# Transposed decode weights go back into their row tile, and the feed-forward's right factors start 192 bytes lower

## The chip, the cores and the metric

The kernel runs on one core of one Trainium2 chip. The metric is the device time of one launch in microseconds (us). A core has a matrix engine (PE, whose weight loads are listed apart as PEld), a vector engine (DVE), a scalar engine (ACT), a general engine (POOL) and a queue processor (SP) that issues nearly all DMA transfers here. Each engine runs its own list of instructions in order, and waits for the others by semaphores. About 0.2% of the time, 3.7 us, is what a measurement of this kernel can tell from no change.

## What is computed

One step of one transformer-like layer over 1024 new frames of a prompt stream and 8 cached streams of 16 new frames each, T = 1152 rows of width 1024, all float32:

```python
def layer(h, p, past, mk, mv):
    mix, st = mixers(rmsnorm(h, p['norm_mix_g']), p, past)
    h = h + mix
    h = h + cross_attend(rmsnorm(h, p['norm_x_g']), mk, mv, p['wq_x'], p['wo_x'])
    h = h + swiglu(rmsnorm(h, p['norm_ffn_g']), p['w_gate'], p['w_up'], p['w_down'])
    return h, st
```

`mixers` projects the rows by `w_in` and runs three mixers side by side: stick-breaking attention (4 heads of 64), a state-space scan (SSD, 8 heads, chunks), and forgetting attention (FoX: softmax attention with cumulated forget gates, 4 heads). The cached streams attend to 1024 past rows, whose keys and values lie in `cache_fox_k`, `cache_fox_v` (and `cache_sb_k`, `cache_sb_v`):

```python
def fox_attend(q, k, v, fq, fk, q_pos, k_pos):
    s = jnp.einsum('bqhd,bkhd->bhqk', q, k) * (HEAD_DIM ** -0.5)
    s = s + (transpose(fq)[..., :, None] - transpose(fk)[..., None, :])
    valid = k_pos[None, :] <= q_pos[:, None]
    p = softmax(where(valid, s, -inf))
    return jnp.einsum('bhqk,bkhd->bqhd', p, v)
```

`swiglu(u)` is `silu(u @ w_gate) * (u @ w_up) @ w_down` with an inner width of 2816.

## The kernel before

The stages follow one another on PE: the memory projection, the norm, the projections by `w_in`, the two attentions (stick-breaking, m = 0; FoX, m = 1) woven with what is left of the projections and then with the SSD chunks, the output projection, cross attention, gate and up, and down. Matrix products of float32 accuracy are made of three matmuls on rounded high and low parts (L341 to L343, and L1918).

No hand-written order: the program text emits the instructions, and a scheduler that simulates the engines chooses each engine's order from the dependencies, the free buffers and priorities. So a change in what holds a buffer moves instructions on all engines, also where their own code is the same.

The buffers that matter here come from pools. `actp` has 6 tiles of 128 x 3072 float32 (`act` in the trace). `wsp` has 7 tiles of 128 x 1152 (`ws`): a tile holds one block of attention rows, that is the scores and then the weights of 128 queries against all keys. `stp` has 8 smaller ones (`st`), and `so` is a pool of 4.

**The cached streams' units.** For each m there are four (p = 0 to 3, two streams each). A unit has a first part `rows` (L869): the queries go in block form into `qt`, cached keys are loaded (L894), transposed on PE (L900) and copied by ACT (L902, `kf`), scores are taken (L885), and the softmax is done (L544 to L555, in a `ws` tile). Its second part `av` (L925) transposes the weights in pieces of 128 x 128 (PE, L936), copies them from PSUM (ACT, L937) to `wt` (past) and `wn` (new rows), and multiplies them with the cached values (loaded by L954; PE, L945). For m = 0 `qt` and `wt` are tiles of `st`, and `wn` a tile of its own; for m = 1 all three are columns of one whole `act` tile, `hold`, which `rows` takes and `av` lets go.

**The SSD scan.** `ssd_gen` (L982) takes one `act` tile, `sc`, for its constants (columns up to 2456), then for each of nine chunks an `act` tile A, into which `load` brings three things: the projected inputs (L1049, `xbcsc`), the cumulated decay spread over all partitions (L1051, `acsc`), and the gate `z` (L1053, `zsc`). ACT and DVE turn the decay into factors (L1089, L1091, L1094), PE multiplies (L1066, L1070, L1081, L1106, L1112, L1151, L1168), and `write` transposes the chunk's output (L1180), copies it (ACT, L1181, `sg`) and stores it (L1182). Other names in the change's neighbourhood: L573, L574, L576 are score matmuls of the prompt's FoX rows, L591 their weights' transposes, L606 their products with the values, L619 the store of these.

**Gate and up** multiply seven sums of the activations (left factors, stationary, `tr`, `tl`, `st`) by seven prepared sums of the normalised rows (right factors `b` and `bT`, moving), 3696 matmuls at L1918, half of them 256 columns wide and half 320. Before the pools of the right factors a small tile `gap` is allocated, so its size shifts the address of everything allocated behind it.

Of the kernel before, what the change touches and what calls it, by code (L numbers as in the profile page):

```python
# [8 lines left out]
F32 = mybir.dt.float32  # L9
# [8 lines left out]
P = 128  # L18
# [5 lines left out]
PAST = 1024  # L24
# [39 lines left out]
def tile_hybrid_step(ctx: ExitStack, tc: tile.TileContext, a: dict):  # L64
# [22 lines left out]
    def act_t(dt=F32R, home=None):  # L87
        return (home or actp).tile([P, 3072], dt, tag="act", name="act")
# [4 lines left out]
    def st_t(dt=F32R):  # L93
        return stp.tile([P, 1024], dt, tag="st", name="st")
# [526 lines left out]
    def sg2_t(dt=F32):  # L621
        return ptp.tile([P, 256], dt, tag="so", name="so", bufs=4)
# [226 lines left out]

    def decode_units(m):
        ck = (a["cache_sb_k"], a["cache_fox_k"])[m][0].rearrange("b k h d -> b k (h d)")
        cv = (a["cache_sb_v"], a["cache_fox_v"])[m][0].rearrange("b k h d -> b k (h d)")
        dmask = dmask_fx if m else dmask_sb
        new = []

        def load_new():

            qsm = st_t(F32).rearrange("p (i x t) -> p i x t", i=4, x=2)  # L860
            SP.dma_start(out=qsm.rearrange("p i x t -> p (i x) t"),
                         in_=f32(qk_sc[4 * m:4 * m + 4, :, :, SEQ:T]).rearrange("i x p t -> p (i x) t"))
            POOL.tensor_tensor(out=qsm[:, :, 0, :], in0=qsm[:, :, 0, :], in1=qsm[:, :, 1, :], op=ALU.add)
            vsm = pt_t(F32)[:, :256].rearrange("p (h x d) -> p h x d", h=4, x=1)
            SP.dma_start(out=vsm.rearrange("p h x d -> p (h x d)"), in_=v_sc[m][SEQ:T, :])
            new.extend((qsm, vsm))

        def rows(p):
            if not new:  # L869
                load_new()  # L870
            qsm = new[0]

            hold = act_t(F32) if m else None
            qt = (hold if m else st_t(F32))[:, 0:P]
            POOL.memset(qt, 0.0)
            q0 = qsm[:, 0:2, 0, 32 * p:32 * p + 32].rearrange("p n (b t) -> p n b t", b=2)
            qp = qt.rearrange("p (b n e t) -> p n e b t", b=2, n=2, e=2)
            for par in range(2):
                r = slice(par * 64, par * 64 + 64)
                for nb in range(2):  # L880
                    POOL.tensor_copy(qp[r, nb, par], q0[r, nb])

            def quads(ps, moving):

                together([lambda g=g: PE.matmul(ps[32 * g:32 * g + 32, :], qt[:, 32 * g:32 * g + 32],  # L885
                                                moving(g // 2, g % 2), start=True, stop=True) for g in (3, 0, 1, 2)])

            def load_k(hf, b2):
                rvs = []
                for q in range(2):  # L890
                    rvs.append(raw_t()[:, :512].rearrange("p (k c) -> p k c", c=256))
                    k0 = hf * 512 + q * 256

                    SP.dma_start(out=rvs[q], in_=ck[2 * p + b2, k0:k0 + 256, :].rearrange("(p k) c -> p k c", k=2))  # L894
                kf = ring.tile([P, 1088], F32, tag=("wh", "wl")[b2], name="kf")
                for q in range(2):
                    tp = pT()
                    for nb in range(2):
                        for k in range(2):
                            PE.transpose(tp[:, (2 * nb + k) * P:(2 * nb + k + 1) * P], rvs[q][:, k, nb * P:(nb + 1) * P],  # L900
                                         ident)
                    ACT.copy(kf[:, :1024].rearrange("c (n q p k) -> c n q p k", n=2, q=2, k=2)[:, :, q],  # L902
                             tp.rearrange("c (n k p) -> c n p k", n=2, k=2))
                return kf

            def emit_past(hf):
                def emit(ps):
                    kf = [load_k(hf, b2) for b2 in range(2)]
                    quads(ps, lambda b2, nb: kf[b2][:, nb * 512:(nb + 1) * 512])
                return emit  # L910

            def emit_new(ps):
                PE.matmul(ps, identr, dmask[:, 96 - 32 * p:224 - 32 * p], start=True, stop=False)
                together([lambda g=g: PE.matmul(ps[32 * g:32 * g + 32, :], qt[:, 32 * g:32 * g + 32], qsm[:, 2 + g % 2, 0, :],
                                                start=False, stop=True) for g in range(4)])

            pieces = [(0, 512, emit_past(0)), (512, 512, emit_past(1)), (1024, P, emit_new)]
            if m == 0:
                return sb_rows(T, pieces), hold
            fkb = xc_t()  # L920
            SP.dma_start(out=fkb[:, :PAST],
                         in_=fs4[8 * p:8 * p + 8].rearrange("r i k -> (r i) k").unsqueeze(1).to_broadcast([32, 4, PAST]))
            return fox_rows(T, pieces, [(0, PAST, fkb[:, :PAST]), (PAST, P, fnew)], fqs[:, p:p + 1], frs[:, p:p + 1]), hold

        def av(p, w, hold):  # L925
            vsm = new[1]

            wt = hold[:, P:P + 1024] if m else st_t(F32)
            wn = hold[:, P + 1024:2 * P + 1024] if m else sg2_t()[:, :P]
            for k0 in (0, 4, 8):  # L930
                nk = min(4, 9 - k0)
                tp = pT()
                for k in range(nk):
                    wk = w[:, 8 * P:9 * P] if k0 == 8 else \
                        w[:, k0 * P:(k0 + 4) * P].rearrange("q (p k) -> q p k", k=4)[:, :, k]
                    PE.transpose(tp[:, k * P:(k + 1) * P], wk, ident)  # L936
                ACT.copy(wn if k0 == 8 else wt[:, k0 * P:(k0 + 4) * P], tp[:, :nk * P])  # L937

            po = pO()

            def quads(w, moving, start, stop):
                def one(g):
                    v = moving(g // 2, g % 2)
                    out = po[32 * g:32 * g + 32, :P]
                    return PE.matmul(out if len(v.shape) == 2 else out.rearrange("p (h d) -> p h d", h=2),  # L945
                                     w[:, 32 * g:32 * g + 32], v, start=start, stop=stop)
                return [lambda g=g: one(g) for g in (3, 0, 1, 2)]

            work = quads(wn, lambda b2, nb: vsm[:, 2 * nb:2 * nb + 2, 0, :], True, False)
            for hf in range(2):  # L950
                raws = []
                for b2 in range(2):
                    raw = ring.tile([P, 1088], F32, tag=("wh", "wl")[b2], name="vr")
                    SP.dma_start(out=raw[:, :1024].rearrange("p (k c) -> p k c", c=256),  # L954
                                 in_=cv[2 * p + b2, hf * 512:(hf + 1) * 512, :]
                                 .rearrange("(p k) c -> p k c", k=4))
                    raws.append(raw)
                for k in range(4):
                    work += quads(wt[:, (4 * hf + k) * P:(4 * hf + k + 1) * P],
                                  lambda b2, nb, raws=raws, k=k: raws[b2][:, k * 256 + nb * P:k * 256 + (nb + 1) * P],  # L960
                                  False, hf == 1 and k == 3)
            together(work)
            ob = sg2_t()[:, :P]
            DVE.scalar_tensor_tensor(ob.rearrange("p (h d) -> p h d", h=2), po[:, :P].rearrange("p (h d) -> p h d", h=2),
                                     frs[:, p:p + 1] if m else 1.0, maskh.unsqueeze(2).to_broadcast([P, 2, 64]),
                                     ALU.mult, ALU.mult)
            of = pT()
            PE.matmul(of[:, :64], ob, fold2.rearrange("p n t -> p (n t)"), start=True, stop=True)
            on = sg2_t()[:, :64]
            DVE.tensor_copy(on, of[:, :64])  # L970
            SP.dma_start(out=mix_sc[2 * m:2 * m + 2, :, SEQ + 32 * p:SEQ + 32 * p + 32].rearrange("n p t -> p n t"),
                         in_=on.rearrange("p (n t) -> p n t", n=2))

        return [([lambda p=p: rows(p)], lambda w, p=p: av(p, *w[0])) for p in range(4)]


    final = []

    def ssd_gen():
        sc = act_t(F32)  # L980
        hT, gB = sc[:, 0:512], sc[:, 512:1024]
        triu, btri, ones, bones = (sc[:, 1024 + 128 * i:1152 + 128 * i] for i in range(4))  # L982
        bmask = sc[:, 1536:1544]
# [736 lines left out]
    tmp = ctx.enter_context(f_pool("tmp", 1))  # L1720
    tlp = ctx.enter_context(f_pool("tlp", NL))
    gap = ctx.enter_context(f_pool("gap", 1))
    gap.tile([P, 56], F32, tag="gap", name="gap")
    bstack = ctx.enter_context(ExitStack())
    slots = [(tlp, "tl")]
    turn = [0]
# [398 lines left out]
```

## Time and profile before

| what | value |
| --- | --- |
| time, median of 3 runs | 1868.5 us (1866.71 to 1868.78) |
| time of the profiled execution | 1863.43 us |
| its span | 1861.7 us |
| mean granted PE clock | 0.992 |
| PE busy | 1804.3 us, 97% |
| DVE / ACT / POOL busy | 897.6 / 796.8 / 619.4 us |
| DMA, mean | 156 GB/s |

A page of the profile gives each engine's busy time, the span in 40 slices (each 46.5 us here) with the busy tenths, the granted clock of PE (9 is 90% or more) and the DMA share, and the chain of work that ended last. Views of the trace give the waits by engine (who waited for what, for how long), the instructions in order of time, and stretches with busy time and clock. In a row of the order of time, equal instructions that follow one another are merged ("x4"), and a bracket shows how long the engine stood idle ahead of them and what ended that. The stretch of the two attentions woven with SSD runs from about 200 to 720 us.

### The profile page before, as it was taken

Reading aid. Unit: us, or ns where it says so; the run is one execution under the profiler, and the core shown is the slowest. Engines: PE = TensorE matmul, PEld = TensorE weight load, DVE = VectorE, ACT = ScalarE, POOL = GpSimd, SP = SyncE. Lnnn points to the kernel's source line nnn. Section 1 sums busy time; section 2 is a strip of 40 time slices with the busy share of each in tenths; the row PEclk is TensorE's granted clock in tenths of the full one; section 3 lists DMA queues with packets and bytes.
Section 4 is the critical chain, followed back from the end, with each engine's and each line's share of the span. In section 5 each row is a group of like instructions: output and inputs, shape, how many; then the busy total and the mean of one; then the engine's idle time right before and its main releaser. Section 6 shows DMA issues by size and latency. Waiting matters only on the chain.

```text
span 1861.7 us, 32061 instructions
## 1 busy us (share of the span) xinstructions
PE 1804.3 (97%) x12008; PEld 1617.0 (87%) x12008; DVE 897.6 (48%) x1792; ACT 796.8 (43%) x1697; POOL 619.4 (33%) x921
## 2 busy tenths in 40 slices
PE   7999999999999999999999989999999999999998
PEld 5899878888966777899988889999999999888886
DVE  3412323476657864455553695333333334455554
ACT  6532544545456862343342564333333333344443
POOL 7622425445215663121021107444444542000000
PEclk9999999999999999999999989999999999999999
DMA  9465645437588883357873124322222223657572
GB/s 337 154 187 149 212 141 142 146 100 211 167 255 265 280 285 109 115 133 168 189 233 111 77 90 116 91 72 71 72 71 72 72 73 93 218 187 249 173 250 85
DMA packets 305547, 289.54 MB, mean 156 GB/s; under 512 B 113004, under 2 KB 257364, under 8 KB 305392
## 3 DMA queue, kind: packets, MB, share of 16 engines
q1 hardware_dynamic: 305392, 287.49, 50.7%
q8 instruction: 95, 1.56, 0.3%
q14 instruction: 60, 0.49, 0.1%
HBM read 221.58 MB, written 66.38 MB: 155 GB/s over the span
## 4 chain that ended last, share of the span: by engine, by line
PE 81%; DMA 6%; DVE 5%; POOL 3%; ACT 2%; issue 2%; SPq 1%; DVEq 0%; POOLq 0%; ACTq 0%
PE psd L1918 11%; PE psd L341 10%; PE psd L342 10%; PE psd L343 10%; PE pst L1918 8%; PE pss L1918 4%; PE pss L341 4%; PE pss L343 4%; PE pss L342 4%; PE pso L1918 2%; PE pst L343 2%; POOL wl L133 2%; PE pst L341 2%; PE pst L342 2%; PE pso L606 1%
## 5 line engine op out<-in xcount | busy, mean ns | idle before, releaser
L133 POOL TENSOR_TENSOR wl<-wr,wh 128x256 fp32r<-128x256 f32 (+2 forms) x152 | 121.2, 829 | 189.0 <-ACT wh L295 178.5
L341 PE MATMUL psd<-act,wh 128*128 128x384 f32 x528 | 182.1, 345 | 0.0
L343 PE MATMUL psd<-act,wl 128*128 128x384 f32 x528 | 180.0, 341 | 0.6 <-POOL wl L133 0.6
L342 PE MATMUL psd<-act,wh 128*128 128x384 f32 x528 | 179.5, 340 | 0.0
L1918 PE MATMUL pst<-bT,tr 128*128 128x256 f32 (+1 forms) x1068 | 155.1, 293 | 0.0
L1918 PEld LDWEIGHTS pst<-bT,tr 128*128 128x128 f32 x1068 | 144.9, 188 | 0.1
L342 PE MATMUL psd<-wl,act 128*128 128x256 f32 (+3 forms) x414 | 133.1, 322 | 2.5 <-POOL wl L133 2.4
L343 PE MATMUL psd<-wh,act 128*128 128x512 f32 (+3 forms) x424 | 135.3, 320 | 0.0
L341 PE MATMUL psd<-wh,act 128*128 128x256 f32 (+3 forms) x414 | 132.3, 323 | 1.8 <-ACT act L1397 1.4
L1918 PE MATMUL psd<-bT,tr 128*128 128x320 f32 (+1 forms) x912 | 132.9, 295 | 0.3 <-POOL tr L133 0.3
L1918 PEld LDWEIGHTS psd<-bT,tr 128*128 128x128 f32 x912 | 124.9, 188 | 0.6 <-POOL tr L133 0.6
L133 POOL TENSOR_TENSOR tr<-u,tr 128x256 fp32r<-128x256 f32 x110 | 82.7, 781 | 101.0 <-ACT tr L1754 83.1
L256 POOL TENSOR_SCALAR sm<-sm 128x1 f32<-128x1 f32 (+2 forms) x27 | 8.9, 330 | 294.7 <-ACT y L2029 206.9
L1893 DVE TENSOR_TENSOR tr<-tr,pst 128x256 f32<-128x256 f32 (+1 forms) x86 | 38.6, 449 | 139.9 <-ACT tr L1890 106.9
L343 PEld LDWEIGHTS psd<-act,wl 128*128 128x128 f32 x528 | 99.3, 188 | 3.1 <-issue 1.7
L133 POOL TENSOR_TENSOR ws<-ws 128x256 f32<-128x256 f32 (+2 forms) x100 | 69.4, 721 | 96.8 <-DVE ws L535 88.5
L341 PEld LDWEIGHTS psd<-act,wh 128*128 128x128 f32 x528 | 99.4, 188 | 2.4 <-issue 1.8
L342 PEld LDWEIGHTS psd<-act,wh 128*128 128x128 f32 x528 | 99.4, 188 | 1.8 <-issue 1.5
L133 POOL TENSOR_TENSOR tr<-raw,tr 128x256 fp32r<-128x256 f32 x94 | 69.3, 767 | 84.4 <-ACT tr L1754 76.2
L1754 ACT CAST tr<-u 128x512 fp32r<-128x512 f32 x130 | 76.7, 620 | 28.5 <-PE pst L1918 5.9
L342 PEld LDWEIGHTS psd<-wl,act 128*128 128x128 f32 x414 | 78.7, 190 | 10.0 <-POOL wl L133 4.3
L341 PEld LDWEIGHTS psd<-wh,act 128*128 128x128 f32 x414 | 78.8, 190 | 9.6 <-ACT act L1397 1.6
(645 smaller groups left out, 4635.4 us busy)
## 6 DMA issues: line engine op xcount, KB each, us to landing
u<-w_down SPq DMA_DIRECT2D x40, 512.0 KB
raw<-w_down SPq DMA_DIRECT2D x26, 512.0 KB
st<-qksc SPq DMA_DIRECT2D x48, 256.0 KB
wr<-w_in SPq DMA_DIRECT2D x44, 256.0 KB
tr<-hidsc SPq DMA_DIRECT2D x55, 192.0 KB
hidsc<-tr SPq DMA_DIRECT2D x34, 288.0 KB
qksc<-sg SPq DMA_DIRECT2D x48, 192.0 KB
wr<-cache_sb_k SPq DMA_DIRECT2D x32, 256.0 KB
```

Source lines behind the costliest of these rows:

```text
L133: POOL.tensor_tensor(out=out[:, a0:a1], in0=in0[:, a0:a1], in1=in1[:, a0:a1], op=op)
L256: POOL.tensor_scalar(v, ss, inv, EPS, ALU.mult, ALU.add)
L341: PE.matmul(out, ah, bh, start=start, stop=False)
L342: PE.matmul(out, ah, bl, start=False, stop=False)
L343: PE.matmul(out, al, bh, start=False, stop=stop)
L606: return PE.matmul(po[r:r + 64, q_], vt[:, 2 * (k0 + i) + j, :], pfs[i][:, sl], start=start and k0 == 0 and (j == 0 or qp > 0), stop=k0 + ...
L1754: ACT.copy(hi, src)
L1893: DVE.tensor_tensor(out=at(out, g), in0=at(x, g), in1=ps[g][:, :GW[g]], op=op)
L1918: PE.matmul(dst[g][:, :GW[g]], x[:, ka], y[:, k, :], start=start and k == 0 and m == 0, stop=stop and k == 3 and m == 2, skip_group_check= ...
```

## The change

Three edits. The FoX units no longer take an act tile: the transposed weights are written back over the row tile `w` from which they were transposed (for both m), and `qt` of the FoX units lies in columns 2456 to 2711 of one act tile (two places, by the parity of p), the same tile that `ssd_gen` then uses for its constants. And the `gap` tile is 8 columns wide, not 56.

```diff
+    kept = []
+
+    def keep_t():
+        if not kept:
+            kept.append(act_t(F32))
+        return kept[0]
+
     def decode_units(m):
...
-            hold = act_t(F32) if m else None
-            qt = (hold if m else st_t(F32))[:, 0:P]
+            qt = keep_t()[:, 2456 + P * (p % 2):2456 + P * (p % 2) + P] if m else st_t(F32)[:, 0:P]
             POOL.memset(qt, 0.0)
...
-        def av(p, w, hold):
+        def av(p, w):
             vsm = new[1]
-
-            wt = hold[:, P:P + 1024] if m else st_t(F32)
-            wn = hold[:, P + 1024:2 * P + 1024] if m else sg2_t()[:, :P]
+            wt, wn = w[:, 0:8 * P], w[:, 8 * P:9 * P]
...
     def ssd_gen():
-        sc = act_t(F32)
+        sc = keep_t()
...
-    gap.tile([P, 56], F32, tag="gap", name="gap")
+    gap.tile([P, LEAD], F32, tag="gap", name="gap")
```

`LEAD` is 8. The right factors of gate and up, and the tiles of the down stage allocated behind them, start 192 bytes lower in each partition: the first at byte 53248, where it was 53440. That is a multiple of 128 bytes now, and was 64 bytes past one.

Because a line number after the change is higher by 4 to 7, L1049 before is L1053 after, L1051 is L1055, L1053 is L1057, L894 is L900, L900 is L906, L1081 is L1085, L1106 is L1110, L1180 is L1184, L1168 is L1172 and L936 is L940; L573 to L619 keep theirs.

Two places of the order. The first is SP's list where the load of the SSD chunk 7 stands, the last before SSD's end; `xbcsc`, `acsc` and `zsc` are its three transfers, `cache_fox_k` and `cache_fox_v` the last FoX unit's, and `waits` names the queues and engines awaited. Before:

```order
L894 DMA wr<-cache_fox_k 128x512 [waits DMAHW4_49,PE_49]
L894 DMA wr<-cache_fox_k 128x512 [waits DMAHW5_49,PE_49]
L894 DMA wr<-cache_fox_k 128x512 [waits DMAHW6_49,PE_49]
L1049 DMA act<-xbcsc 128x8x128 [waits DMAHW7_49,Pool_49]
L619 DMA mixsc<-so 64x256 [waits DMAHW0_49,DVE_49]
L1051 DMA act<-acsc 128x1024 [waits DMAHW1_49]
L1053 DMA act<-zsc 128x512 [waits DMAHW2_49]
L954 DMA vr<-cache_fox_v 128x1024 [waits DMAHW3_49]
```

After:

```order
L900 DMA wr<-cache_fox_k 128x512 [waits DMAHW4_49,PE_49]
L900 DMA wr<-cache_fox_k 128x512 [waits DMAHW5_49,PE_49]
L1053 DMA act<-xbcsc 128x8x128 [waits DMAHW6_49,Pool_49]
L1055 DMA act<-acsc 128x1024 [waits DMAHW7_49]
L1057 DMA act<-zsc 128x512 [waits DMAHW0_49]
L900 DMA wr<-cache_fox_k 128x512 [waits DMAHW1_49,PE_49]
```

The store L619, which awaits DVE, stood between the chunk's first and second transfer; now the three stand together, and one key load stands behind them.

The second is PE's list ahead of the same chunk's product L1106, from the end of the product L1168 of the chunk before. Before:

```order
L1180 MATMUL psd<-identr,sg 128x128 x2
L573 MATMUL pss<-st 128x384
L574 MATMUL pss<-st 128x384
L576 MATMUL pss<-mask_fx,identr 128x128
L1180 MATMUL psd<-identr,sg 128x128 x2
L900 MATMUL pst<-identr,wr 128x128
L591 MATMUL pst<-identr,ws 128x128 x2
L900 MATMUL pst<-identr,wr 128x128
L1081 MATMUL psd<-act 128x128 x2
L573 MATMUL pss<-st 128x512
L574 MATMUL pss<-st 128x512
L1106 MATMUL psd<-act 128x256 x2
```

After:

```order
L1184 MATMUL psd<-identr,sg 128x128 x2
L573 MATMUL pss<-st 128x512
L574 MATMUL pss<-st 128x512
L1184 MATMUL psd<-identr,sg 128x128 x2
L906 MATMUL pst<-identr,wr 128x128 x7
L573 MATMUL pss<-st 128x512
L574 MATMUL pss<-st 128x512
L576 MATMUL pss<-mask_fx,identr 128x128
L1085 MATMUL psd<-act 128x128 x2
L906 MATMUL pst<-identr,wr 128x128 x4
L1110 MATMUL psd<-act 128x256 x2
```

Eleven key transposes now stand between the chunk's output transposes and L1110, where two key and two weight transposes stood.

More of the change, by code (lines that the diff above doesn't have):

```diff
@@ L918, in rows @@
             if m == 0:
-                return sb_rows(T, pieces), hold
+                return sb_rows(T, pieces)
             fkb = xc_t()
@@ L922, in rows @@
                          in_=fs4[8 * p:8 * p + 8].rearrange("r i k -> (r i) k").unsqueeze(1).to_broadcast([32, 4, PAST]))
-            return fox_rows(T, pieces, [(0, PAST, fkb[:, :PAST]), (PAST, P, fnew)], fqs[:, p:p + 1], frs[:, p:p + 1]), hold
-        def av(p, w, hold):
+            return fox_rows(T, pieces, [(0, PAST, fkb[:, :PAST]), (PAST, P, fnew)], fqs[:, p:p + 1], frs[:, p:p + 1])
+        def av(p, w):
             vsm = new[1]
-            wt = hold[:, P:P + 1024] if m else st_t(F32)
-            wn = hold[:, P + 1024:2 * P + 1024] if m else sg2_t()[:, :P]
+            wt, wn = w[:, 0:8 * P], w[:, 8 * P:9 * P]
             for k0 in (0, 4, 8):
@@ L972, in av @@
                          in_=on.rearrange("p (n t) -> p n t", n=2))
-        return [([lambda p=p: rows(p)], lambda w, p=p: av(p, *w[0])) for p in range(4)]
+        return [([lambda p=p: rows(p)], lambda w, p=p: av(p, w[0])) for p in range(4)]
     final = []
     def ssd_gen():
-        sc = act_t(F32)
+        sc = keep_t()
         hT, gB = sc[:, 0:512], sc[:, 512:1024]
```

## The prediction

> **What bounds the kernel now.** I began with the page's busy times, which name the engine that sets the end.
>
> ```profile
> span 1861.7 us, 32061 instructions
> PE 1804.3 (97%) x12008; PEld 1617.0 (87%) x12008; DVE 897.6 (48%) x1792; ACT 796.8 (43%) x1697; POOL 619.4 (33%) x921
> PEclk9999999999999999999999989999999999999999
> ```
>
> PE is busy 97% of the span, so a change can win only by shortening PE's idle time, its time at a low granted clock, or the spacing of its matmuls. What moves on ACT and POOL (43% and 33% busy) costs nothing while PE has other work in its list. The diff keeps the number of matmuls and of transfers in all stages, so the second view is the stretches in which the order differs, with columns from and to, length, PE busy, granted clock, DMA share, GB/s.
>
> ```profile
> core 0: us, PE busy (x), PEclk, DMA share, GB/s
> 500.00:550.00 50.00, 46.74 (x417) 1.00 0.87 261
> 550.00:600.00 50.00, 44.85 (x334) 1.00 0.83 267
> 600.00:650.00 50.00, 48.85 (x472) 1.00 0.84 281
> 650.00:700.00 50.00, 47.23 (x349) 0.93 0.82 282
> 1300.00:1400.00 100.00, 100.00 (x758) 1.00 0.26 67
> ```
>
> In the FoX and SSD stretch PE is idle for 3.3 + 5.2 + 1.2 + 2.8 = 12.5 us of 200, and it is here that the order differs. The last row is gate and up: no idle at all, so there only the spacing of matmuls can change. The third view, PE's waits from 500 to 710 us, says what ended that idle time (total, times, longest).
>
> ```profile
> PE psd L1106 <- ACT sg L1181: 2.7, 1, 2.7
> PE psd L1180 <- DVE sg L1175: 1.8, 1, 1.8
> PE pst L900 <- DMA wr<-cache_fox_k: 1.8, 1, 1.8
> PE psd L1066 <- DMA act<-xbcsc: 1.7, 2, 1.4
> PE psd L1180 <- DVE st L1334: 1.7, 1, 1.7
> PE pso L945 <- ACT act L937: 1.2, 1, 1.2
> ```
>
> No wait is long. What the change could give is therefore a few microseconds, unless gate and up's spacing moves.
>
> **The held act tile.** SP's own waits between 500 and 670 us show where the hold told before.
>
> ```profile
> SPq L1049 <- PE pso L945: 9.6, 2, 7.1
> ```
>
> Twice the load of an SSD chunk stood at the head of SP's list until a FoX unit's value product (L945) let its act tile go, 9.6 us in all, with every later transfer behind it. The change lifts that. It is worth only what PE waited for those transfers, and the chunk whose data came late enough to stop PE is the one loaded at 651.92. Its steps in order of time, by SP, ACT and PE:
>
> ```profile
> 651.92 0.38 SPq L1049 DMA_DIRECT2D act<-xbcsc  x1
> 653.83 0.45 SPq L619 DMA_DIRECT2D mixsc<-so  x1
> 654.33 0.58 SPq L1051 DMA_DIRECT2D act<-acsc  x1
> 660.34 0.98 ACT L1089 ACTIVATE act<-act 128x128 f32<-128x128 f32 x3 [3.37 <-DMA act<-acsc]
> 661.23 0.56 ACT L1181 COPY sg<-psd 128x512 f32<-128x512 f32 x1
> 661.94 2.04 PE L1106 MATMUL psd<-act 128*128 128x256 f32 x4 [2.72 <-ACT sg L1181]
> ```
>
> The store L619 stood between the chunk's first and second transfer and waited for DVE. ACT then waited 3.37 us for the spread decay, the output copy L1181 lay behind it on ACT, and PE, which needed the PSUM that this copy empties, stopped for 2.72 us. In the new order L1055 follows L1053 at once: 654.33 − (651.92 + 0.38) = 2.0 us earlier. On PE eleven key transposes instead of four other transposes stand just ahead of L1110, and four of them take
>
> ```profile
> 519.56 0.63 PE L900 MATMUL pst<-identr,wr 128*128 128x128 f32 x4 [1.81 <-DMA wr<-cache_fox_k]
> ```
>
> 0.63 us, or (0.63 − 0.27) / 3 = 0.12 us each behind the first, so seven more give 0.8 us of cover. 2.0 + 0.8 = 2.8 covers 2.72, barely: **−2.7 us**. Its bounds are 0 (the transfer is late for another reason) and −2.7.
>
> **The clock.** Just behind that stop the granted clock halves:
>
> ```profile
> 655.00:660.00 5.00, 4.22 (x33) 1.00 1.01 336
> 660.00:664.00 4.00, 2.06 (x6) 0.66 1.03 393
> 664.00:668.00 4.00, 4.00 (x15) 0.50 0.43 129
> 668.00:672.00 4.00, 4.00 (x31) 0.99 0.94 363
> ```
>
> PE worked 2.06 + 4.00 us at half speed, which lost 1.03 + 2.00 = 3.0 us. In the whole stretch from 500 to 700 us no other row but the one with this stop is below 1.00, so I take the stop as the cause and the loss as gone with it: **−3.0 us**, bounds 0 and −3.0.
>
> The Trainium skill, "TensorE: Matmul & The Clock Gate", section "Why this matters for your kernels", says that a gap of PE beyond about 3 us brings the half clock back; this gap was 2.72 us, so the rule speaks for another cause of the drop, and by it this term would be 0 and the sum below −3.9. The trace differs from the rule in that the drop began beside a gap shorter than it names.
>
> **The first FoX unit.** Before, its value product stopped for the last weight copy:
>
> ```profile
> 541.12 0.99 ACT L1089 ACTIVATE act<-act 128x128 f32<-128x128 f32 x3 [2.29 <-DMA act<-acsc]
> 544.96 0.26 ACT L937 COPY act<-pst 128x128 f32<-128x128 f32 x1
> 545.28 0.43 PE L945 MATMUL pso<-pt,act 128*32 128x128 f32 x8 [1.17 <-ACT act L937]
> ```
>
> The copy was late because ACT had itself waited 2.29 us for a chunk's decay. The copies are as many and as long as before, only into the row tile; they are behind the same kind of ACT work. Bounds 0 and −1.2; nothing shows which, so half: **−0.6**. The key load's 1.81 us (quoted above) has the same bounds in kind, 0 to −1.8: SP now sends that unit's key loads ahead of other transfers, but they still share the queues, whose share is 0.87 there. Half again: **−0.9**.
>
> **The row tile is kept longer.** Before, a `ws` tile was free when its last transpose ended; now it is free when the value product ends. The third unit gives the size:
>
> ```profile
> 637.94 0.33 PE L936 MATMUL pst<-identr,ws 128*128 128x128 f32 x1
> 639.87 1.93 PE L945 MATMUL pso<-vr,act 128*32 128x128 f32 x64
> ```
>
> (639.87 + 1.93) − (637.94 + 0.33) = 3.5 us longer, for one of seven tiles, four times. Who waits is the next block's first writer of a row tile (ACT, L544, or DVE from PSUM), and behind it on DVE and ACT the softmax steps, and then PE's transposes L591. No wait for a row tile stands among PE's waits of the trace, so the pool has some slack, which hides it; without it each of four units would cost 3.5. Bounds 0 and +14. I take one unit at half: **+1.8**. The stick-breaking units have the same copies back, but their stretch keeps nearly the whole order, so I give them nothing; the tile of `st` and the small one that each no longer takes are spare there. The queries' move costs nothing: the same memset and copies run on POOL (33% busy), and a place is used again only two units later.
>
> **The addresses.** The 3696 matmuls of gate and up read the same numbers of columns, from a start that is a multiple of 128 bytes instead of 64 past one. The nearest row with 256 columns and such a start (by allocation) is a projection's; I set its spacing beside gate and up's, merged over 12:
>
> ```profile
> 505.14 0.28 PE L343 MATMUL psd<-wh,act 128*128 128x256 f32 x1
> ...
> 507.59 0.28 PE L343 MATMUL psd<-wh,act 128*128 128x256 f32 x1
> ...
> 1309.74 1.58 PE L1918 MATMUL pst<-bT,tr 128*128 128x256 f32 x12
> ...
> ```
>
> The first two are the ends of 22 matmuls in a row: 2.45 / 21 = 116.7 ns from start to start. The third is (1.58 − 0.28) / 11 = 118.2 ns. If all of the 1.5 ns is the start, and the 320 columns gain as much, it is 3696 × 1.5 ns = −5.5 us. The other bound: the durations by shape say no difference, and a loss as large as the gain isn't excluded, since no row tells a start's effect by itself: +5.5.
>
> ```profile
> L1918 PE MATMUL pst<-bT,tr 128*128 128x256 f32 x612 | 84.0, 281 | 0.0
> L342 PE MATMUL psd<-wl,act 128*128 128x256 f32 x144 | 40.5, 281 | 0.0
> ```
>
> 281 ns in both, and the two loops differ in the stationary side and in PSUM as well, so I take about a quarter of the gain: **−1.5**.
>
> By the Trainium skill, "SBUF — State Buffer", section "Specifications (TRN2)", SBUF is read in lines of 16 bytes; a move by 192 is twelve whole lines, so that by it this term is 0 and the sum 1.5 us smaller; no run shows either yet.
>
> **The sum.** −2.7 − 3.0 − 0.6 − 0.9 + 1.8 − 1.5 = −6.9 us. The profiled execution took 1863.43 us, 1.7 beyond its span, so 1856.5 is its counterpart; it was 5.1 us faster than the median of the runs, 1868.5, whose counterpart is 1861.6. I predict the median: **1861.6**, with its own range 1858 to 1865.
>
> **The rivals.**
>
> (B) *The stop moves but stays.* The chunk's decay comes 2 us earlier only if its first transfer is issued no later, and eleven transposes that need key loads may wait for these loads themselves. Then stop and half clock remain (or come at another chunk), and −0.6 − 0.9 + 1.8 − 1.5 = −1.2 is left: 1867.3. For it: the DMA share of 1.01 at 655 to 660, where the queues are full whatever the order. Against it: L619 alone delayed the issue by 2.0 us.
>
> (C) *The start of the right factors is worth its whole 1.5 ns.* −5.4 for the rest and −5.5: 1857.6. For it: the two spacings. Against it: equal durations.
>
> (D) *Slower: row tiles run short.* In the FoX stretch seven row tiles serve the prompt's blocks and the units. If the tile that is free 3.5 us later is the one that the next block waits for, then each of the four units pays 1.8 us or more, from the first of them on, +7.1, and the chunk's copies on ACT come late behind the waiting block, so that stop and clock stay. With −0.6 − 0.9 that is +5.6: 1874.1. For it: ACT and DVE work in order, and a wait blocks what is behind. Against it: no such wait is seen before, and the scheduler's order counts with the tile's real release.
>
> (E) *The change does not do what it says* in the FoX stretch: the act tile is free, but SP's list is bound by something else; this is B's time, and counted there.
>
> **How the numbers follow.** Forecast 0.40, B 0.23, C 0.20, D 0.15, and 0.02 for addresses that cost. A measurement tells about 0.2%, 3.7 us, from no change: faster is below 1864.8, slower above 1872.2. Faster gets C and the forecast but for 0.03: 0.57. Same gets B and that 0.03: 0.26. Slower 0.17. The range reaches from 1855 (C with the second half of the first unit's and key load's waits) to 1872 (D in a mild form), and leaves out the worst of D and of C, about 0.17.
>
> **What would show it.** In the changed kernel's profile, PE's stop ahead of L1110 should be gone, and the granted clock from 600 to 700 us 1.00; if 0.93 remains, B. No SP wait of L1053 on PE L949 should be above 2 us. If ACT or DVE wait for PE's L949 ahead of L544, D, and more than 2 us of it would make the prediction wrong. And twelve merged matmuls of 256 columns in gate and up should take between 1.56 and 1.58 us; 1.56 in nearly all is C, 1.60 the opposite.

## The result, and the profile after

| what | before | changed |
| --- | --- | --- |
| median of 9 runs each | 1866.71 us (1861.98 to 1871.74) | 1876.56 us (1873.19 to 1884.84) |
| ratio, 95% interval | 1 | 1.006 [1.0043, 1.0076] |
| profiled execution | 1863.43 us, span 1861.7 | 1873.19 us, span 1871.3 |
| mean granted PE clock | 0.992 | 0.986 |

The change makes the kernel slower by 0.6%, some 10 us; 1861.6 us, that is faster, was forecast, with 1872 as the upper end. (The median of the kernel before was 1868.5 us over the first three runs and is 1866.71 us over nine.) The page of the changed kernel:

```profile
span 1871.3 us, 32043 instructions
PE 1808.0 (97%) x12008; PEld 1620.5 (87%) x12008; DVE 902.6 (48%) x1792; ACT 796.9 (43%) x1697; POOL 623.0 (33%) x921
PEclk9999999999988999999999989999999999999999
```

The same work, and a new dip of the granted clock in the two slices from 515 to 608 us. Where the 9.6 us of span came from is read at a point behind which both kernels have the same order, the first score matmul of cross attention, first in the kernel before and then in the changed one:

```profile
822.00 0.40 PE L341 MATMUL pss<-kt,st 128*128 128x256 f32 x2
```

```profile
833.54 0.40 PE L341 MATMUL pss<-kt,st 128*128 128x256 f32 x2
```

In these two executions all of the loss, 11.5 us, lies ahead of this point; gate and up, behind it, gave 1.7 us back (504.8 us from its first matmul to its last before, 503.1 now). The stretches, in the columns that the prediction used:

```profile
500.00:550.00 50.00, 47.37 (x428) 0.97 0.99 302
550.00:600.00 50.00, 43.45 (x251) 0.80 0.76 235
600.00:650.00 50.00, 46.45 (x408) 1.00 0.70 232
650.00:700.00 50.00, 46.80 (x392) 1.00 0.81 278
1300.00:1500.00 200.00, 200.00 (x1521) 1.00 0.29 75
```

The half clock that stood at 661 us is gone (1.00, was 0.93). In its place the clock is 0.80 from 550 to 600 us, which was 1.00, and 0.97 ahead of that. PE's idle time from 500 to 700 us is 2.63 + 6.55 + 3.55 + 3.20 = 15.9 us, where it was 12.3 (3.26 + 5.15 + 1.15 + 2.77; the prediction added rounded terms to 12.5). PE's longest waits between 480 and 740 us (total, times, longest):

```profile
PE pst L906 <- DMA wr<-cache_fox_k: 3.6, 1, 3.6
PE pst L940 <- ACT sg L1147: 2.6, 1, 2.6
PE pst L906 <- ACT sg L1185: 2.0, 1, 2.0
PE psd L1110 <- DVE act L1087: 1.8, 2, 1.2
```

The stop of 2.72 us ahead of L1106 is now 2.0 us a little earlier in the same chunk. The other two waits that the prediction priced, for the first FoX unit's keys and for its last weight copy, are gone: the rows of that unit show no idle time there. But two stops are new: 2.6 us ahead of the first FoX unit's last weight transpose, and 3.6 us for a key load of the second.

For the comparisons below I worked out, from windows of 2 us between 480 and 760 us of each profile, PE's idle time (2 us less the busy time) and the time lost at half clock (half of the busy time that falls in it). One profile each, so a single row here is one execution; e1 has the order of the kernel before on every engine, and e2 that of the changed one, and their rows show how far two executions of one order lie apart.

| kernel | idle, us | lost at half clock, us | span, us |
| --- | --- | --- | --- |
| before | 14.0 | 3.1 | 1861.7 |
| e1 order of before | 12.3 | 3.4 | 1860.7 |
| changed | 17.4 | 10.7 | 1871.3 |
| e2 order of changed | 21.4 | 13.7 | 1886.5 |
| e3 row tiles alone | 17.8 | 9.2 | 1872.9 |
| e5 stick-breaking tiles alone | 21.4 | 19.4 | 1886.9 |
| e7 order by the clearing | 13.4 | 11.9 | 1869.0 |
| e9 changed, full rows | 16.9 | 4.5 | 1864.0 |
| e12 and keys first | 16.9 | 5.4 | 1866.6 |

Idle time explains 3.4 us of the changed kernel's loss, the half clock 7.6; the sum, 11.0, is nearly the 11.5 read above. Both e2 and the changed kernel lie above both e1 and the kernel before in the two columns.

### The profile page after: what moved, and what is told of

The parts are those of the page before. It is cut to its first block, busy times and chain, and to the rows that moved or that the text cites. A ratio compares the mean times of both kernels' runs of the same rounds, so it can differ in the third digit from the quotient of the medians.

```text
span 1871.3 us, 32043 instructions
## 1 busy us (share of the span) xinstructions
PE 1808.0 (97%) x12008; PEld 1620.5 (87%) x12008; DVE 902.6 (48%) x1792; ACT 796.9 (43%) x1697; POOL 623.0 (33%) x921
## 4 chain that ended last, share of the span: by engine, by line
PE 80%; DVE 6%; DMA 6%; ACT 2%; issue 2%; POOL 2%; SPq 1%; DVEq 0%; POOLq 0%; ACTq 0%
PE psd L1922 11%; PE psd L341 10%; PE psd L342 9%; PE psd L343 9%; PE pst L1922 8%; PE pss L1922 3%; PE pss L341 3%; PE pss L342 3%; PE pss L343 3%; PE pso L1922 2%; PE pst L343 2%; PE pst L341 2%; PE pst L342 2%; PE pso L606 2%; DMA act<-acsc 1%
## 5 line engine op out<-in xcount | busy, mean ns | idle before, releaser
L133 POOL TENSOR_TENSOR wl<-wr,wh 128x256 fp32r<-128x256 f32 (+2 forms) x152 | 125.1, 857 | 198.7 <-ACT wh L295 184.8
```

The lines of the kernel that those rows point to most:

```text
L133: POOL.tensor_tensor(out=out[:, a0:a1], in0=in0[:, a0:a1], in1=in1[:, a0:a1], op=op)
```

## The experiments

Theories at the start: R, which is rival D of the prediction (row tiles are kept longer and run short); T, the freed act tile lets SSD work begin earlier, into full queues; and that the addresses cost. Behind the first four runs came O: no one buffer, but any new order of this stretch brings other stops, and half clock with them. Ratios are to the kernel before, by runs on the same chip.

### The addresses alone, and the tiles alone

```diff
-    gap.tile([P, 56], F32, tag="gap", name="gap")
+    gap.tile([P, LEAD], F32, tag="gap", name="gap")
```

> The kernel before with the gap tile of 8 columns alone; every engine's list is the same as before, only the right factors of gate and up lie 192 bytes lower. Theory (a start at a multiple of 128 bytes speeds the 256-column matmuls by about 1.7 ns and leaves the 320-column ones): 1848 x 1.7 = 3.1 us less, some 1863.5 against 1866.7, ratio 0.998 to 0.999. Rival (the spacing in the changed kernel comes from something else in it): ratio 1.000.

The second run is the changed kernel with 56 there.

> The changed kernel with the gap tile of 56 columns as before; every engine's list is that of the changed kernel. Theory (the whole loss lies in the new order of the FoX and SSD stretch, which the addresses only lessened): +11 to +13 us, ratio 1.006 to 1.007, slower than the changed kernel by 2 to 3 us. Rival (the addresses of the right factors or of the tiles behind them cost part of it): ratio nearer 1.003 to 1.005.

Measured: e1 0.9991 [0.9978, 1.0003], 1866.32 us against 1868.93; e2 1.0071 [1.0052, 1.0091], 1881.14 us against the same. The tiles carry the whole loss, as e2's theory had it. For e1 the ratio can't tell a gain from none; the stage of gate and up can: 504.8 to 505.8 us in the ten profiles with a gap of 56, 504.1 to 504.5 in the six with 8 named next. So the addresses give a little back, less than the 3.1 us expected. By the spacing from start to start, mean over all 256-column matmuls of gate and up under 160 ns: 118.3 ns with a gap of 56 (ten profiles, all within 0.03), 117.7 with 8 in six profiles (e1, e9, e10, e12, e15, e16), and 116.6 in the changed kernel's one profile; 320 columns keep 146.7 or 146.8 in all. 0.6 ns x 1848 is 1.1 us. Rows of twelve merged matmuls, of e1, e2 and the changed kernel in this order:

```profile
1309.44 1.58 PE L1918 MATMUL pst<-bT,tr 128*128 128x256 f32 x12
```

```profile
1312.35 1.58 PE L1922 MATMUL pst<-bT,tr 128*128 128x256 f32 x12
```

```profile
1321.26 1.56 PE L1922 MATMUL pst<-bT,tr 128*128 128x256 f32 x12
```

Why the changed kernel's profile stands 1.1 ns below the other profiles with the same addresses isn't explained.

### Which tile

Row tiles kept as in the change, act tiles held as before:

```diff
-            wt = hold[:, P:P + 1024] if m else st_t(F32)
-            wn = hold[:, P + 1024:2 * P + 1024] if m else sg2_t()[:, :P]
+            wt, wn = w[:, 0:8 * P], w[:, 8 * P:9 * P]
```

> The kernel before with the transposed weights back in the row tile for both mixers, and the FoX units still holding an act tile each (for the queries alone); gap of 56. Row tiles are kept as long as in the changed kernel, act tiles as long as before. Rival D of the prediction (row tiles run short): +5 to +11 us, ratio 1.003 to 1.006. Theory (the freed act tile lets the SSD begin earlier, into full queues): within 3 us of before, ratio 0.999 to 1.0015.

The changed kernel with the stick-breaking units as before (56 columns of gap):

```diff
-            wt, wn = w[:, 0:8 * P], w[:, 8 * P:9 * P]
+            wt = w[:, 0:8 * P] if m else st_t(F32)
+            wn = w[:, 8 * P:9 * P] if m else sg2_t()[:, :P]
```

> The changed kernel with the stick-breaking units' transposed weights in their own tiles as before; gap of 56. Act tiles are free as in the changed kernel. Theory (freed act tile): most of the loss stays, ratio 1.004 to 1.007. Rival (the stick-breaking units' longer hold of row tiles sets the loss): ratio 1.000 to 1.002.

Measured: e3 1.0058 [1.0042, 1.0074]; e4 1.0049 [1.0032, 1.0065]. R's run was slow as R had it, T's run as T had it (e4 also keeps the FoX units' row tiles longer, so it isn't T by itself); each part of the change costs about what the whole costs. That fits neither as a sum, and led to O and the next four.

The stick-breaking units alone, in the kernel before:

```diff
-            wt = hold[:, P:P + 1024] if m else st_t(F32)
-            wn = hold[:, P + 1024:2 * P + 1024] if m else sg2_t()[:, :P]
+            wt = hold[:, P:P + 1024] if m else w[:, 0:8 * P]
+            wn = hold[:, P + 1024:2 * P + 1024] if m else w[:, 8 * P:9 * P]
```

> The kernel before with the transposed weights back in the row tile for the stick-breaking units alone; the FoX units as before, gap of 56. It differs from the run of the row tiles alone by the FoX units' row tiles. Theory R (row tiles kept longer by the FoX units cost): ratio within 0.9985 to 1.0015. Theory O (no one resource: a new order of the FoX and SSD stretch brings other stops of PE and half clock with it, and the order before had few of them): ratio 1.001 to 1.005, as this one's order too differs from before's.

The freed act tile alone, in the changed kernel with a gap of 56:

```diff
-            wt, wn = w[:, 0:8 * P], w[:, 8 * P:9 * P]
+            wt, wn = st_t(F32), sg2_t()[:, :P]
```

> The changed kernel with the transposed weights of all units in tiles of their own (those that the stick-breaking units had before), so that act tiles are free as in the changed kernel and row tiles as early as before; gap of 56. Theory R: ratio 0.997 to 1.0015, since only the freed act tile is left. Theory T (the freed act tile lets SSD begin earlier, into full queues): 1.004 to 1.007. Theory O: slower too, 1.002 to 1.007, without a common wait.

Two orders without any change of a buffer, in the kernel before:

```diff
-            POOL.memset(qt, 0.0)
+            (DVE if m else POOL).memset(qt, 0.0)
```

> The kernel before with the clearing of the FoX units' query tile on DVE, not on POOL: four instructions of some 0.1 us, no buffer held longer or shorter; the order of the FoX and SSD stretch changes in some places by it (some 390 lines of PE's list). Theories R and T: ratio 0.999 to 1.001. Theory O: 1.001 to 1.005.

```diff
-RATE = (1.0, 1.1, 60)
+RATE = (1.0, 1.08, 60)
```

> The kernel before with SSD pieces emitted at 1.08 a step of the attention pipeline, not 1.10: the same instructions and buffers, another order from the second FoX unit on. Theories R and T: ratio 0.999 to 1.0015. Theory O: 1.001 to 1.006, with other stops of PE in the profile and half clock behind some of them.

| run | ratio | interval |
| --- | --- | --- |
| e5 stick-breaking tiles alone | 1.0123 | 1.0107 to 1.0139 |
| e6 act tile freed alone | 1.0042 | 1.0024 to 1.0061 |
| e7 clearing on DVE | 1.0031 | 1.0018 to 1.0045 |
| e8 rate 1.08 | 1.0034 | 1.0015 to 1.0053 |

e5 lost twice what the whole change lost, although the whole change contains it: that is above the expectation of R and also above that of O (at most 1.005), and a cost per tile can't give it. e6 refuses R as the only cause, e5, in which the act tiles are held as before, T. And e7 and e8, in which every buffer is held as before, lost 0.3% each. So a new order by itself can cost this much, by its stops and half clock, and the kernel before has an order with few of them. That a buffer adds a smaller cost of its own isn't excluded by these four.

### What the clock answers to

In e7 the half clock has no stop ahead of it. Its windows from 540 us (busy, clock, DMA share), and all of PE's waits between 525 and 575 us:

```profile
540.00:545.00 5.00, 4.63 (x47) 1.00 0.60 132
545.00:550.00 5.00, 5.00 (x73) 1.00 0.39 116
550.00:555.00 5.00, 5.00 (x18) 0.65 0.87 261
555.00:560.00 5.00, 5.00 (x21) 0.50 1.08 293
560.00:565.00 5.00, 5.00 (x18) 0.50 0.54 166
565.00:570.00 5.00, 5.00 (x18) 0.50 0.42 131
```

```profile
PE pso L945 <- ACT act L937: 0.4, 1, 0.4
PE pso L606 <- ACT pt L594: 0.2, 1, 0.2
```

From 545 us on PE is busy all through, waits 0.6 us in 50, and still runs at half clock for 20.5 us. What it does there are the cached streams' products, the costliest groups from 545 to 572 us:

```profile
L1151 PE MATMUL pst<-act 32*128 32x256 f32 x16 | 6.8, 545 | 0.0
L1151 PE MATMUL psd<-act 32*128 32x256 f32 x12 | 6.2, 613 | 0.0
L1141 PE MATMUL pst<-identr,act 128*128 128x128 f32 x16 | 3.9, 423 | 0.0
L1144 PE MATMUL psd<-sg,act 128*32 128x256 f32 x16 | 3.8, 634 | 0.0
```

L1151 (L1155 after the change), the update of the SSD states, uses 32 of the array's 128 rows, L1144 and the value product 32 of its columns. So theory H: a stretch of such thin matmuls counts as little used for the clock; its rival G: the stop of 2.6 us ahead of that stretch in the changed kernel is the cause. In the next three runs the 32 products are made over all rows, the moving side masked to zero outside the two streams, with the same results and, on every engine, the same order (but for at most four of DVE's 1792 instructions); the first is the changed kernel with it:

```diff
-                    bm = (A, B)[g][:, 2560:2816]
-                    POOL.tensor_tensor(out=bm.rearrange("p (e n) -> p e n", n=P),
-                                       in0=Bn[:, g * P:(g + 1) * P].unsqueeze(1).to_broadcast([P, 2, P]),
-                                       in1=maskh.unsqueeze(2).to_broadcast([P, 2, P]), op=ALU.mult)
+                    bm = [(A, B)[h][:, 2560:3072] if g == 0 else st8[h][:, 2304:2816] for h in range(2)]
+                    for h in range(2):
+                        POOL.tensor_tensor(out=bm[h].rearrange("p (b n) -> p b n", n=P),
+                                           in0=Bn[:, g * P:(g + 1) * P].unsqueeze(1).to_broadcast([P, 4, P]),
+                                           in1=bmask[:, 4 * h:4 * h + 4].unsqueeze(2).to_broadcast([P, 4, P]), op=ALU.mult)
...
-                            pss_[x][:, :256], xe[r:r + 32, j * P:(j + 1) * P], bms[j // 2][r:r + 32, :],
+                            pss_[x][:, :256], xe[:, j * P:(j + 1) * P], bms[j // 2][hf][:, 256 * x:256 * x + 256],
```

> The changed kernel with the 32 thin products of the cached streams' state update (L1155, 32 of the 128 rows of the array each) made over all 128 rows, with the moving side masked to zero outside the two streams (4 POOL operations of 512 columns instead of 2 of 256); same results, same order on every engine. Theory H (in the stretch around 550 us the clock halves because thin matmuls and short stops together leave PE's array too little used, not for one long stop): half clock between 545 and 575 us gone or one window of 3.4 us, ratio to before 1.002 to 1.004 instead of 1.006. Rival G (the stop of 2.6 us ahead of it is the cause): half clock there as before, 10 to 14 us, ratio 1.005 to 1.008.

> The kernel before with the gap tile of 8 columns and the same full-row products; the order on every engine is that of before. Theory H: the executions of the kernel before that fall to half clock there lose it, ratio 0.9975 to 0.999. Rival G: as the gap alone, 0.998 to 1.000.

> The run with the clearing on DVE, with the full-row products; its profile had 20.5 us of half clock from 551.5 to 572 us and no stop of PE over 0.4 us in the 25 us ahead of it. Theory H: half clock there gone or one window, ratio 0.999 to 1.001 instead of 1.003. Rival G: nothing to say on it, since there is no stop; if full rows change nothing, ratio 1.002 to 1.004.

And the same in e5:

> The run with the stick-breaking units' weights back in the row tile alone (ratio 1.0123, the slowest), with the full-row products, order unchanged. Its profile had 13.6 us of half clock between 546 and 566.5 us, which cost 6.4 us, and some 13 us lost by stops and half clock from 580 us on. Theory H: ratio 1.007 to 1.010, the rest at its other stops. If full rows do nothing here: 1.011 to 1.0135.

| run | without full rows | with full rows |
| --- | --- | --- |
| changed, e9 | 1.0060 [1.0043, 1.0076] | 1.0025 [1.0009, 1.0042] |
| gap alone, e10 | 0.9991 [0.9978, 1.0003] | 0.9996 [0.9980, 1.0011] |
| clearing on DVE, e11 | 1.0031 [1.0018, 1.0045] | 1.0011 [1.0000, 1.0021] |
| stick-breaking tiles, e13 | 1.0123 [1.0107, 1.0139] | 1.0095 [1.0067, 1.0122] |

The stretch in the changed kernel, and then in e9:

```profile
540.00:545.00 5.00, 2.37 (x13) 0.81 1.13 244
545.00:550.00 5.00, 5.00 (x91) 0.85 0.88 301
550.00:555.00 5.00, 4.26 (x26) 0.83 0.01 4
555.00:560.00 5.00, 3.65 (x13) 0.50 0.58 133
560.00:565.00 5.00, 5.00 (x20) 0.50 1.07 265
```

```profile
540.00:545.00 5.00, 3.70 (x34) 1.00 1.11 301
545.00:550.00 5.00, 3.50 (x80) 1.00 0.41 152
550.00:555.00 5.00, 3.74 (x15) 1.00 0.08 17
555.00:560.00 5.00, 4.64 (x34) 1.00 1.10 250
560.00:565.00 5.00, 5.00 (x28) 1.00 1.11 295
```

In these 25 us PE is idle for 4.4 us in e9 and for 4.7 us in the changed kernel, and the clock stays whole in e9 alone. Of H's expectations e9's and e13's held; e11's ratio came out 0.0001 above its range; e10's failed and lies in G's range, since no half clock was to be lost there, and none was gained. e13's interval overlaps that of e5; the clock from 546 to 566 us, 0.67 in e5 and 0.91 in e13, says the same. But G isn't refused as a whole. PE's stop ahead of the first unit's last weight transpose, in e9 and in e12 (the next run, also with full rows):

```profile
540.75 0.33 PE L940 MATMUL pst<-identr,ws 128*128 128x128 f32 x1 [1.14 <-ACT sg L1147]
```

```profile
545.39 0.47 PE L940 MATMUL pst<-identr,ws 128*128 128x128 f32 x1 [5.78 <-ACT sg L1147]
```

The same stop was 2.63 us in the changed kernel, 1.14 in e9. At the 5.78 us of e12 the clock is half from 542.5 to 549.3 us, with full rows.

The clock's records allow a count that joins both. In all 18 traces the half clock lasts 3.41 us or a multiple of it (but for the one cut off by the end of the run), so I divided each trace into such windows. In each between 480 and 760 us I summed the time of PE's matmuls, each weighted by the part of the 128 rows that it uses, and looked at the clock of the window behind it:

| weighted share, window at full clock | windows | half clock next |
| --- | --- | --- |
| below 0.40 | 25 | 25 |
| 0.40 to 0.60 | 51 | 23 |
| 0.60 to 0.70 | 50 | 1 |
| above 0.70 | 1261 | 0 |

Once at half clock, it stayed there behind all 27 windows with a share below 0.80, and behind 10 of the 55 above 0.90. By PE's plain busy time six windows above 0.70 are followed by half clock, all between 548 and 561 us and in kernels without full rows (in e7 one is busy all through, with a weighted share of 0.53); weighted by columns there are again six above 0.70. So rows count here, idle time counts too, and the thin columns of L1144 and of the value product don't explain it. In the changed kernel the 3.4 us from 543.1 us follow a window of 0.38, which is the stop, and the 13.7 us from 553.3 us one of 0.60 (busy 0.88), which is thin matmuls for the most part.

It also shows where chance enters. The kernel before has windows of 0.52 and 0.54 in this stretch and kept the whole clock; e7 halved behind 0.53. And the stop ahead of L1106 in e1, whose order is that of before,

```profile
661.97 1.10 PE L1106 MATMUL psd<-act 128*128 128x256 f32 x4 [2.07 <-ACT sg L1181]
```

falls across two windows (0.67 and 0.72), and no half clock follows; in the kernel before it was 2.72 us, mostly inside one window (0.40).

### The key loads

What was left of e9's loss was a stop with half clock behind it, SP's rows, PE's, and the window (busy, clock) behind it:

```profile
571.88 0.38 SPq L1053 DMA_DIRECT2D act<-xbcsc  x1
572.35 0.54 SPq L619 DMA_DIRECT2D mixsc<-so  x1
572.94 0.58 SPq L1055 DMA_DIRECT2D act<-acsc  x1
573.57 0.49 SPq L1057 DMA_DIRECT2D act<-zsc  x1
574.16 0.85 SPq L900 DMA_DIRECT2D wr<-cache_fox_k  x2
```

```profile
580.90 1.11 PE L906 MATMUL pst<-identr,wr 128*128 128x128 f32 x4 [3.85 <-DMA wr<-cache_fox_k]
```

```profile
580.00:590.00 10.00, 9.10 (x42) 0.50 1.06 384
```

The second FoX unit's key loads stand behind all three transfers of an SSD chunk, which is loaded this early in the new order. Moving them up:

```diff
+                    with tc.high_priority(200) if m else nullcontext():
-                    SP.dma_start(out=rvs[q], in_=ck[2 * p + b2, k0:k0 + 256, :].rearrange("(p k) c -> p k c", k=2))
+                      SP.dma_start(out=rvs[q], in_=ck[2 * p + b2, k0:k0 + 256, :].rearrange("(p k) c -> p k c", k=2))
```

> The changed kernel with the full-row products (run e9_full_rows_changed, ratio 1.0025) and, on top, the FoX units' key loads at a higher priority, so that two of them stand ahead of the second transfer of an SSD chunk's load in SP's list and no longer behind all three. Theory K (what is left of the loss is the stop of 3.8 us for a key load near 577 us, and the half clock behind it): the stop at 2 us or less, half clock behind it one window or none, ratio 0.9985 to 1.001. Rival O (a stop removed there comes back elsewhere in the stretch): ratio 1.001 to 1.004.

Measured: 0.9982 [0.9965, 1.0000], 1866.09 us against 1867.66. The stop is gone, and with it the half clock behind it (the same three views of e12):

```profile
576.87 1.01 SPq L900 DMA_DIRECT2D wr<-cache_fox_k  x2
```

```profile
578.12 0.60 PE L906 MATMUL pst<-identr,wr 128*128 128x128 f32 x4
```

```profile
580.00:590.00 10.00, 9.51 (x84) 1.00 1.06 352
```

e9's and e12's intervals don't meet, so this edit takes away the second half of the loss, and the ratio is a little below K's range. That the late keys alone were this half isn't shown: the edit also moves some 430 of PE's 12008 instructions, and the two profiles don't show the gain (e9's profiled execution took 1865.95 us, below its median of 1871.41, and e12's 1868.34, above its median; idle and half clock together are 21.4 and 22.3 us). In e12's profile a stop came back elsewhere, the 5.78 us above, as rival O had it. At this one place theory T fits: an early chunk load delays the keys behind it.

### The last stop, and the tile change without its stops

The remaining long stop is that ahead of the first unit's last weight transpose. ACT in the changed kernel, and PE behind it:

```profile
542.94 0.59 ACT L1147 COPY sg<-pst 128x512 f32<-128x512 f32 x1 [3.55 <-DMA st<-qksc]
543.58 0.47 PE L940 MATMUL pst<-identr,ws 128*128 128x128 f32 x1 [2.63 <-ACT sg L1147]
```

In e12 it was 5.78 us, and ACT's wait is put down to the store of z (`zsc<-sg`), which reads the staging tiles `sg` that L1147 needs; so is the same wait in e2, though the row above names another transfer. Hence, on top of e12:

```diff
-                            h0.append(sg_t())
+                            h0.append(pt_t(F32))
```

> The run e12_keys_first (changed kernel, full-row products, key loads first; ratio 0.9982) with the copies of the cached states (ACT, L1147) in tiles of another pool, whose contents no store reads, not in the staging tiles that the store of z (L810) must have read first. SP's list is the same, ACT's differs in a few rows around these copies. Theory S (the stop of 2.6 us in the changed kernel and 5.8 us in that run ahead of the first FoX unit's weights comes from ACT waiting for such a store): stop under 1 us, ratio 0.995 to 0.998. Rival O: a stop of the same size elsewhere, ratio 0.998 to 1.001.

And the kernel before with the same four edits beside the tiles:

> The kernel before with the same four edits as the run above beside the tile change: gap of 8, full-row products, key loads first, copies in the other pool. If the row tiles and the freed act tile are worth nothing by themselves: the same ratio as the run above within 0.0015. If the freed act tile helps once the three stops are gone: the run above is lower by 0.002 or more. If row tiles run short: this one is lower by 0.002 or more.

Measured: e15 1.0001 [0.9987, 1.0016]; e16 1.0010 [0.9996, 1.0024]. In e15 that stop is gone, but the ratio is above theory S's range: another stop has come 7 us later, and 10.2 us of half clock from 549.7 us with it, in spite of the full rows. ACT's row, PE's, and the window (busy, clock):

```profile
549.88 0.99 ACT L1093 ACTIVATE act<-act 128x128 f32<-128x128 f32 x3 [4.84 <-DMA act<-acsc]
552.19 0.69 PE L972 MATMUL pst<-fold,so 128*128 128x64 f32 x2 [4.26 <-DVE so L968]
```

```profile
550.00:560.00 10.00, 7.18 (x17) 0.50 0.15 36
```

The first chunk's decay arrives at 549.9 us, and my reading is that until then PE runs out of other work at one instruction or another: rival O. e15 and e16 agree within 0.0009, so beside these four edits the tile change shows no gain and no loss. Their orders differ too, so a small worth of the tiles that one order hides isn't excluded. No version beats the kernel before with certainty; the two lowest are e12 (0.9982, up to 1.0000) and e1 (0.9991, up to 1.0003).

### The addresses, once more

A gap of 16 columns, one profile:

> The kernel before with a gap tile of 16 columns: the right factors start 32 bytes past a multiple of 128. If only a start at a multiple of 128 bytes is fast, gate and up's 256-column matmuls are at 118.5 ns on average and the stage at 504.5 to 505.5 us, as with 56; if the spacing follows something else, it can be nearer the 503 to 504 us of the two profiles with a gap of 8.

256 columns at 117.8 ns, 320 at 146.7, the stage 504.3 us: as with 8 columns in e1 (504.3), though this start is no multiple of 128 bytes. So the start at 64 bytes past such a multiple is the slower one here; a rule for all starts isn't shown.

## Why the prediction was wrong

**What bounds the kernel.** Right: in the two profiles the loss lies in the FoX and SSD stretch and is PE's stops and half clock, 11.0 us of 11.5.

**The stop ahead of L1106, −2.7.** Its cause was named rightly and its size was not. The two transfers stand together now, but the decay still came 7.1 us after its issue (667.97 to 675.12), where it had taken 6.0, and the stop was 2.0 us: −0.7.

**The clock, −3.0.** This is the step that failed. The term was to be −3.0 us, and the time lost at half clock rose from 3.1 to 10.7 us, +7.6. From 600 to 700 us the clock was whole, as forecast; that proves little, since in e1 and e10, with the order of before, no half clock lay behind that stop either (in e14, of the same order, 3.4 us did). The sentence "I take the stop as the cause and the loss as gone with it" treated half clock as the tail of one long stop. The count above shows what stands in its place: the half clock follows a window of 3.4 us in which PE's rows are little used, by stops or by matmuls of few rows. The stretch with most of these lay ahead at 545 to 572 us at whole clock, with a window down to 0.54 of use, and I never priced what it would cost if it lost that: 6 to 10 us in the profiles of the changed kernel and of e7. e9 and e11, with the same orders and full rows, have no half clock there. The Trainium skill, "TensorE: Matmul & The Clock Gate", section "Why this matters for your kernels", which the prediction set against this term, speaks of idle gaps near 3 us; e7 halved with no gap over 0.4 us, so the measurement goes beyond the page. The same page of the Trainium skill, section "Part 1: The HAM clock gate (the "warmup" mystery)", gives the window of that clock as 3413 ns; the half clocks read above lasted 3.4, 6.8, 10.2, 13.7 and 20.5 us, which agrees.

**The first unit, −0.6, and the key load, −0.9.** The two waits went wholly, so by themselves these terms were at their lower bounds, −1.2 and −1.8. What failed beside the clock is that the sum had no term for a new stop: 2.63 us came ahead of the first unit's last weight transpose and 3.60 us for the second unit's keys, and PE's idle time rose by 3.4 us (14.0 to 17.4), where all terms of stops together gave −4.2 and the row tile +1.8. I had let the new order take waits away in three places and looked for new ones in none.

**The row tile, +1.8, and rival D.** D had the sign and nearly the size (1874.1 against 1876.6; its sum left out the −1.5 of the addresses, with which it is 1872.6). That was luck, since the runs don't bear its mechanism out: e6, without the longer hold, is slower too, e5 with half of it is the slowest, and e16, with none, equals e15 within the intervals. The profile has one longer wait of the kind, DVE's for a row tile, but a prompt block's transposes end it, not a unit's value product (L949):

```profile
DVE ws L548 <- PE pst L591: 3.2, 1, 3.2
```

It was 0.6 us before; what it costs isn't measured apart. D's chance should have gone to a rival of another kind, an order with more stops.

**The addresses, −1.5.** The gain in the stage was 1.7 us in the two profiles and, by e1's spacing, 1.1; the profiles with one gap or the other differ by 0.3 to 1.7. Sign and size held, and a term of 0 did not, by the spacing. C's full 5.5 did not.

**The lower and upper end.** What the range lacked is that an order that a scheduler makes anew is itself a draw: e7 and e8 moved nothing but order (in e7 also four clearings of some 0.1 us) and cost 0.3%. Its lower end is 1856.1 by the terms named for it, not 1855.

## What to carry to other kernels

Where a scheduler makes the order, price an edit against a neutral edit that also makes the order anew, before giving its buffers the credit or the blame. List the stretches where the matrix engine runs matmuls of few rows at whole clock, since there a small delay can cost several microseconds at half clock (6 to 10 us here), and give such matmuls full rows where masking is cheap; against long stops that doesn't help (e12, e15). A buffer that comes free earlier also sends its loads earlier: look at what stands behind them in the queue. And take several executions of one order before a half clock in one profile is priced.

## What the runs showed of the hardware that was not expected

PE's clock halved for 20.5 us while PE was busy all the time, on matmuls with 32 rows (e7), and did not where the same products ran over 128 rows with PE idle for 4.1 us of 15 (e9, 540 to 555 us). Counted over 18 traces from 480 to 760 us, each window of 3.4 us whose use of PE's rows was below 0.40 was followed by half clock (25), and none above 0.70 was (1261). And a moving operand of 256 columns was read at 118.3 ns from a start 64 bytes past a multiple of 128, at 117.7 and 117.8 from starts 0 and 32 bytes past one (116.6 in one profile at 0, unexplained), while 320 columns took 146.7 or 146.8 ns in all three.
